# The layout of 2 KB of row scales on their way through DRAM, in a one-core decoder layer

## The chip, the cores and the metric

The kernel runs on one core of one Trainium2 chip, in one launch. The metric is the device time of an execution in microseconds, lower is better. Its engines are named as in the profile: PE (TensorE, matrix products; PEld is its weight load), DVE (VectorE), ACT (ScalarE), POOL (GpSimd) and SP (SyncE, which in this kernel issues every DMA transfer).

## The reference

One decoder layer over 2048 tokens of width 1024, float32. An input projection feeds two groups: a differential attention of 8 heads, and a gated linear recurrence of the same width. Their outputs, each with a SiLU gate, are joined, projected, normalised and added to the input. The change touches the end of the attention only, the RMS norm of each head's output over its 128 channels (the sub-norm):

```python
def rmsnorm(x, g):
    xf = x.astype(jnp.float32)
    y = xf * lax.rsqrt(jnp.mean(xf * xf, axis=-1, keepdims=True) + NORM_EPS)
    return (y * g.astype(jnp.float32)).astype(x.dtype)
...
o = diff_attention(qh, kh, vh, lam)
o = rmsnorm(o, subln_g[l]) * (1.0 - lam_init)
y_attn = o.reshape(B, S, ATTN_WIDTH).astype(x.dtype) * jax.nn.silu(g_attn)
...
y = jnp.concatenate([y_attn, y_lru], axis=-1)
y = jnp.einsum('bse,ed->bsd', y, w_out[l])
x = x + rmsnorm(y, post_norm_g[l])
```

So every (token, head) pair has one scale, the reciprocal root, by which 128 values are multiplied.

## The kernel before, in words

Matmuls take each float32 operand as a high and a low part, and three products replace one (`hi*hi`, `lo*hi`, `hi*lo`). The work runs in five stages.

1. Up to about 590 us: normalise and transpose the input, then project (L228, L530) and run the recurrence for tokens 0 to 1023. Everything that later stages need is stored in DRAM: `q_s`, `k_s`, `v_s`, `g_s`, `yl_s`.
2. To about 1125 us: `attention` for the token pairs 0 to 3 (a pair is 256 tokens), all 8 heads, with the projections of tokens 1024 to 2047 (`fill_proj`) woven in as filler for PE.
3. To about 1390 us: the recurrence of the second half; `load_wo` loads and splits the first blocks of `w_out`.
4. To about 2203 us: `attention` for pairs 4 to 7, with the output projection as filler (`fill_out`, L1048). It loads `y` from `ya_s` or `yl_s` (L958), splits it on POOL (L70, L71), loads partial sums (`part_s`, L1036 to L1044), adds them on DVE (L1058, one PSUM tile for all groups) and, for rows that are complete, runs `finish`: squares on ACT (L972), a product on POOL (L973), a reciprocal root on DVE (L979, L86 to L97), the residual (L983) and the store (L986). When the block of `w_out` changes, `load_wo` (L950) loads eight new pieces through two buffers, each split by POOL.
5. The rest: the output projection of the last 1024 rows (`right`, `left`, L1098).

`attention` goes through a list of slots, one per (head, pair, half, component). For each slot an order is written out by hand: loads of keys, values, queries and gates (L600, L606, L616, L623), the softmax exponentials (L683), then matmuls by a small clock model: scores (L642), transposes of the weights (L715, then ACT L719 and DVE L720), values (L738) and filler; last `combine` and the norm steps. The norm of a (head, 512 tokens) is cut into six steps over five slots: norm1 takes the squares on ACT and `yt`, the gated output, on DVE (L751); norm2 sums the squares over channels on PE (L760) and takes the reciprocal root on DVE (L75 to L82, called `f` in the profile). There the scales lie as 128 partitions x 4, token `t*128 + q` at partition q, column t, whereas `yt` has channels on its partitions and tokens along them. So the scales must be laid out along the free dimension and repeated on all 128 partitions. This is done through DRAM: norm3 (L773) writes 2 KB to `r_s`, norm4 (L777) reads them back with the same 2 KB for every partition into `rb`, norm5 (L782) multiplies on POOL, norm6 (L785) stores the result in `ya_s`. There are 8 heads x 4 = 32 such norms, 16 in stage 2 and 16 in stage 4.

All DMAs are issued by SP in the order in which the program states them. L777 waits there until the write of L773 has landed, and L785 until POOL's product is done.

Of the kernel before, what the change touches and what calls it, by code (L numbers as in the profile page):

```python
# [8 lines left out]
F32 = mybir.dt.float32  # L9
# [4 lines left out]
ALU = mybir.AluOpType  # L14
# [4 lines left out]
P = 128  # L19
# [3 lines left out]
H = 8  # L23
CH = 512
NJ = S // CH
# [18 lines left out]
def hymba_kernel(  # L44
# [6 lines left out]
    nc = tc.nc  # L51
# [5 lines left out]
    def grid(name, shape, a, b):  # L57
        return [[dram.tile(shape, F32, name=f"{name}{i}_{j}") for j in range(b)] for i in range(a)]
# [2 lines left out]
    k_s = grid("k_s", [64, 2, 2, CH], H, NJ)  # L61
    v_s = grid("v_s", [P, 2, 4, CH], 2, NJ)
    g_s = grid("g_s", [P, CH], H, NJ)
    r_s = grid("r_s", [4, P], H, NJ)
    ya_s = [dram.tile([P, H, CH], F32, name=f"ya_s{j}") for j in range(NJ)]
    yl_s = [dram.tile([P, NB, CH], F32, name=f"yl_s{j}") for j in range(NJ)]
    part_s = [[dram.tile([P, D], F32, name=f"part_s{r}_{i}") for i in range((8, 16)[r])] for r in range(2)]
# [524 lines left out]
    def attention(prs, kv_p, e_p, a_p, ps_s, ps_w, ps_o, nsb, fill, per_slot, kbufs, vbufs, p1bufs):  # L592
# [151 lines left out]
        nrm = {}  # L744
# [25 lines left out]
            nrm[h, j] = (f, yt)  # L770

        def norm3(h, j):
            nc.sync.dma_start(out=r_s[h][j].rearrange("t q -> q t"), in_=nrm[h, j][0][:, 2, :])  # L773

        def norm4(h, j):
            rb = a_p.tile([P, 4, P], F32, tag="sq", name="rb", bufs=1)
            nc.sync.dma_start(out=rb, in_=r_s[h][j].partition_broadcast(P))  # L777
            nrm[h, j] = (rb, nrm[h, j][1])

        def norm5(h, j):  # L780
            rb, yt = nrm[h, j]
            nc.gpsimd.tensor_tensor(out=yt, in0=yt, in1=rb.rearrange("p t q -> p (t q)"), op=ALU.mult)  # L782

        def norm6(h, j):
            nc.sync.dma_start(out=ya_s[j][:, h, :], in_=nrm.pop((h, j))[1])  # L785
# [9 lines left out]
        for p in range(H * NS):  # L795
            h, pr = p // NS, prs[p % NS]
# [35 lines left out]
        for s in range(U + 12):  # L832
# [49 lines left out]
            run("N1", norm1)  # L882
            run("N2", norm2)
            run("N3", norm3)
            run("N4", norm4)
            run("N5", norm5)
            run("N6", norm6)
        for _ in fill:
# [12 lines left out]
    with ExitStack() as pa:  # L901
        kv_p = pa.enter_context(tc.tile_pool(name="kvA", bufs=2))
        e_p = pa.enter_context(tc.tile_pool(name="expA", bufs=2))
        a_p = pa.enter_context(tc.tile_pool(name="attA", bufs=2))
# [106 lines left out]
    with ExitStack() as pb:  # L1011
        kvB_p = pb.enter_context(tc.tile_pool(name="kvB", bufs=2, side="right"))
        e_p = pb.enter_context(tc.tile_pool(name="expB", bufs=2, side="right"))
        a_p = pb.enter_context(tc.tile_pool(name="attB", bufs=2, side="right"))
# [153 lines left out]
```

## Time and profile before

| | |
|---|---|
| median of 3 runs | 2303.52 us (2302.61 to 2305.75) |
| profiled execution, its own time | 2302.22 us |
| its span, first to last instruction | 2300.4 us |
| granted clock of PE, mean | 0.98 |
| busy: PE, DVE, ACT, POOL | 2183.5, 1482.6, 984.2, 804.7 us |
| moved by DMA | 317.94 MB, 138 GB/s |

In rows of the profile, `x32` is a count; a row of a timeline gives start, duration, engine, line, operation and `out<-in`, and in square brackets how long the engine was idle before it and who ended that. A row of waits gives the total, the number of times and the longest. A row of a time window gives the window, its length, the busy time of PE, PEld, DVE, ACT and POOL, the granted clock, the busy share of the DMA engines and their GB/s. "DMA to landing" is the time from a transfer's issue to its completion.

### The profile page before, as it was taken

To read this page: it belongs to the slowest core of one execution; us is meant where nothing else is said; L and a number is where in the kernel's file an instruction comes from. 1 tells how busy PE (TensorE), PEld (TensorE's weight loads), DVE (VectorE), ACT (ScalarE), POOL (GpSimd) and SP (SyncE) were. 2 spreads that over 40 slices of the span, in tenths; PEclk is the share of its full clock that TensorE was granted. 3 is DMA by queue.
4 is the path that set the end of the run, shared out by engine and by line. 5 is a ranking of instruction groups with operands and counts; after the bars stand their busy time and mean duration, and the time that the engine had idled before them with its cause. 6 is when DMAs were issued, how large, how long until landed. Compare 5 with 4: busy or idle time off the path is not lost. (4 is left out here: it accounts for less than half of the span.)

```text
span 2300.4 us, 31837 instructions
## 1 busy us (share of the span) xinstructions
PE 2183.5 (95%) x11281; PEld 1800.9 (78%) x11281; DVE 1482.6 (64%) x2976; ACT 984.2 (43%) x2227; POOL 804.7 (35%) x773
## 2 busy tenths in 40 slices
PE   7999999999899999999989998999999998999778
PEld 6888888888678878888878775888788886887666
DVE  6532145456576666666237786888888887888565
ACT  4311134434443444444125564665555655555211
POOL 1222034444311111111266553233533335345452
PEclk9999999999999999999999998999999999999989
DMA  6554322332569876864452117456466475655473
GB/s 201 155 150 149 112 86 85 105 106 69 141 155 188 169 172 175 183 165 116 128 179 67 60 37 185 105 138 169 112 156 165 111 147 135 173 138 142 113 258 128
DMA packets 358785, 317.94 MB, mean 138 GB/s; under 512 B 32546, under 2 KB 290659, under 8 KB 358627
## 3 DMA queue, kind: packets, MB, share of 16 engines
q1 hardware_dynamic: 358626, 315.91, 52.8%
q8 instruction: 89, 1.46, 0.3%
q14 instruction: 70, 0.57, 0.1%
HBM read 221.41 MB, written 94.44 MB: 137 GB/s over the span
## 5 line engine op out<-in xcount | busy, mean ns | idle before, releaser
L228 PE MATMUL ps<-hh,whi 128*128 128x512 f32 (+1 forms) x1456 | 569.6, 391 | 2.7 <-DVE hilo L245 2.0
L228 PE MATMUL ps<-hh,wlo 128*128 128x512 f32 (+1 forms) x1456 | 567.4, 390 | 0.0
L228 PE MATMUL ps<-hl,whi 128*128 128x512 f32 (+1 forms) x1456 | 565.2, 388 | 1.1 <-DVE hl L446 1.1
L683 ACT ACTIVATE p<-s,nm 128x512 f32<-128x512 f32 (+3 forms) x640 | 392.1, 623 | 328.7 <-DVE nm L667 220.4
L665 DVE TENSOR_REDUCE mx<-s 128x1 f32<-128x512 f32 (+3 forms) x576 | 341.0, 617 | 114.9 <-PE s L642 96.3
L642 PE MATMUL s<-ks,qs 128*128 128x512 f32 (+2 forms) x1280 | 369.7, 387 | 28.9 <-DMA ks<-k_s 16.8
L200 POOL TENSOR_TENSOR wlo<-wraw,whi 128x1024 fp32r<-128x1024 f32 x88 | 222.7, 2531 | 437.3 <-DVE whi L199 133.3
L228 PEld LDWEIGHTS ps<-hh,whi 128*128 128x128 f32 x1456 | 277.6, 191 | 53.6 <-DVE hilo L245 2.4
L228 PEld LDWEIGHTS ps<-hl,whi 128*128 128x128 f32 x1456 | 277.2, 190 | 52.7 <-DVE hl L446 1.4
L228 PEld LDWEIGHTS ps<-hh,wlo 128*128 128x128 f32 x1456 | 276.6, 190 | 51.1
L642 PEld LDWEIGHTS s<-ks,qs 128*128 128x128 f32 x1280 | 216.4, 192 | 82.3 <-ACT p L683 33.0
L719 ACT ACTIVATE wh<-pw 128x512 fp32r<-128x512 f32 (+1 forms) x288 | 160.3, 577 | 186.5 <-PE pw L715 183.0
L738 PE MATMUL o<-wh,vs 128*128 128x256 f32 (+1 forms) x1152 | 222.5, 283 | 0.0
L720 DVE TENSOR_TENSOR wl<-pw,wh 128x512 fp32r<-128x512 f32 (+1 forms) x288 | 185.4, 653 | 35.8 <-ACT wh L719 34.3
L738 PEld LDWEIGHTS o<-wh,vs 128*128 128x128 f32 x1152 | 193.2, 191 | 18.1 <-ACT wh L719 2.1
L70 POOL TENSOR_SCALAR yh<-yraw 128x256 fp32r<-128x256 f32 x196 | 92.3, 488 | 290.6 <-PE f L1048 267.9
L1048 PE MATMUL f<-woh,yh 128*128 128x512 f32 x392 | 163.2, 416 | 25.0 <-DVE yv L1058 17.9
L782 POOL TENSOR_TENSOR yt<-yt,rb 128x512 f32<-128x512 f32 x32 | 44.1, 1379 | 405.4 <-DMA rb<-r_s 218.7
L701 DVE SCALAR_TENSOR_TENSOR p<-p,rr,p 128x128 f32<-128x128 f32 (+15 forms) x128 | 179.2, 1400 | 2.8
L715 PE MATMUL pw<-ident,p 128*128 128x128 f32 x1088 | 169.4, 274 | 5.8 <-DVE wl L720 4.5
L738 PE MATMUL o<-wl,vs 128*128 128x256 f32 x576 | 163.7, 284 | 8.9 <-DVE wl L720 8.9
L1048 PE MATMUL f<-wol,yh 128*128 128x512 f32 x392 | 163.3, 417 | 0.9 <-POOL wol L71 0.9
(166 smaller groups left out, 3298.7 us busy)
## 6 DMA issues: line engine op xcount, KB each, us to landing
wraw<-in_w_in_dram SPq DMA_DIRECT2D x96, 512.0 KB, 4.8
qs<-q_s SPq DMA_DIRECT2D x128, 256.0 KB, 5.2
vs<-v_s SPq DMA_DIRECT2D x48, 512.0 KB, 6.2
ks<-k_s SPq DMA_DIRECT2D x96, 256.0 KB, 5.5
xt<-in_x_dram SPq DMA_DIRECT2D x32, 512.0 KB, 4.7
k_s<-hilo SPq DMA_DIRECT2D x64, 256.0 KB, 4.2
q_s<-hilo SPq DMA_DIRECT2D x64, 256.0 KB, 3.5
v_s<-hilo SPq DMA_DIRECT2D x32, 512.0 KB, 3.7
```

The costliest lines, as they stand in the source:

```text
L70: nc.gpsimd.tensor_scalar(out=hi, in0=src, scalar1=1.0, scalar2=1.0, op0=ALU.mult, op1=ALU.mult)
L200: nc.gpsimd.tensor_tensor(out=lo, in0=src, in1=hi.bitcast(F32), op=ALU.subtract)
L228: nc.tensor.matmul(out=ps[:, t0:t0 + n], lhsT=a[:, k, :], rhs=b[:, k, t0:t0 + n], start=(k == 0 and m == 0), stop=(k == KC - 1 and m == 2),)
L642: nc.tensor.matmul(out=ps[:, b0 - c0:b0 - c0 + nk], lhsT=qq[:, c, t * P:(t + 1) * P], rhs=kst[h, b0 // CH][:, c, 0:nk], start=(m == 0), st ...
L665: nc.vector.tensor_reduce(out=mx[:, pi:pi + 1], in_=sc[u, pi][:, 0:c1 - c0], axis=AX.X, op=ALU.max)
L683: nc.scalar.activation(out=p[:, c0:c1], in_=sc.pop((u, pi))[:, 0:c1 - c0], func=AF.Exp, bias=negm[u], accum_out=acc,)
L701: nc.vector.scalar_tensor_tensor(out=p0[:, 0:n], in0=p1[:, 0:n], scalar=rr[:, 1:2], in1=p0[:, 0:n], op0=ALU.mult, op1=ALU.add,)
L715: nc.tensor.transpose(pw[:, i * P:(i + 1) * P], wts[h, pr, t][:, kb * P:(kb + 1) * P], ident)
L719: nc.scalar.activation(out=wh[:, 0:n], in_=pw[:, 0:n], func=AF.Copy)
L720: nc.vector.tensor_tensor(out=wl[:, 0:n], in0=pw[:, 0:n], in1=wh[:, 0:n].bitcast(F32), op=ALU.subtract,)
L738: nc.tensor.matmul(out=po[h, j][:, oo:oo + w1 - w0], lhsT=a[:, kb % 4, :], rhs=w[:, w0:w1], start=(kb == 0 and m == 0), stop=(kb == 2 * pr ...
L1048: nc.tensor.matmul(out=ps, lhsT=a[:, k, :], rhs=b, start=(k == 0 and m == 0), stop=(k == 7 and m == 2),)
```

## The change

`r_s` becomes partition-major: [128, 4] in place of [4, 128]. The write then puts the four scales of a partition next to one another, 16 bytes in one run; before, each scale went to a place 512 bytes from the next of its partition. The broadcast read is again 2 KB in one run per partition, but `rb` now holds them as 128 x 4, so the product on POOL reads `rb` with a step of four elements. `yt` stays as it is, seen as 4 x 128.

```diff
-    r_s = grid("r_s", [4, P], H, NJ)
+    r_s = grid("r_s", [P, 4], H, NJ)
...
         def norm3(h, j):
-            nc.sync.dma_start(out=r_s[h][j].rearrange("t q -> q t"), in_=nrm[h, j][0][:, 2, :])
+            nc.sync.dma_start(out=r_s[h][j], in_=nrm[h, j][0][:, 2, :])

         def norm4(h, j):
-            rb = a_p.tile([P, 4, P], F32, tag="sq", name="rb", bufs=1)
+            rb = a_p.tile([P, P, 4], F32, tag="sq", name="rb", bufs=1)
             nc.sync.dma_start(out=rb, in_=r_s[h][j].partition_broadcast(P))
             nrm[h, j] = (rb, nrm[h, j][1])

         def norm5(h, j):
             rb, yt = nrm[h, j]
-            nc.gpsimd.tensor_tensor(out=yt, in0=yt, in1=rb.rearrange("p t q -> p (t q)"), op=ALU.mult)
+            y4 = yt.rearrange("p (t q) -> p t q", t=4)
+            nc.gpsimd.tensor_tensor(out=y4, in0=y4, in1=rb.rearrange("p q t -> p t q"), op=ALU.mult)
```

## The prediction

> **What bounds the kernel now.** I read the page first (busy shares, transfers, chain), then the SyncE queue's own waits, then the rows of the two lines that the change touches, and last the timelines around every idle stretch of TensorE (PE) that can be followed back to them.
>
> ```profile
> PE 2183.5 (95%) x11281; PEld 1800.9 (78%) x11281; DVE 1482.6 (64%) x2976; ACT 984.2 (43%) x2227; POOL 804.7 (35%) x773
> ...
> DMA packets 358785, 317.94 MB, mean 138 GB/s; under 512 B 32546, under 2 KB 290659, under 8 KB 358627
> ...
> PE ps_y L1098 3%; DMA r_s<-f 1%; DMA yraw<-ya_s 1%; DMA out_dram<-xt 0%; DMA yv<-part_s 0%; DVE w3l L204 0%; DMA rb<-r_s 0%; PE f L1048 0%; DMA xt<-in_x_dram 0%; DVE xt L983 0%; DVE w3h L203 0%; DVE f L81 0%; PE s L642 0%; DVE f L82 0%; DVE f L80 0%
> ```
>
> PE is busy 2183.5 us; against the span of 2300.4 us that leaves 117 us in which it idles; but for the pace of the matmuls themselves, no change of transfers can win more. The share lines of the chain name a tiny transfer, `r_s<-f` (2 KB), second.
>
> The SyncE queue's waits, in total, times, longest:
>
> ```profile
> SPq L777 <- DMA r_s<-f: 242.2, 32, 9.8
> ...
> SPq L785 <- POOL yt L782: 163.5, 32, 8.2
> ```
>
> SyncE issues every transfer in program order. Per norm (32 of them) it stands 242.2 / 32 = 7.6 us at L777 until the write of L773 has landed, because the broadcast read needs it, and 5.1 us more at L785 for the product. Everything later in the program that must be loaded stands behind.
>
> The rows of the lines, durations in ns and the landing times of their transfers:
>
> ```profile
> L773 SPq DMA_DIRECT2D r_s<-f x32: 367/376/1200, 661.3 to 2173.6; - x32
> ...
> DMA to landing us min/median/max: 7.6/9.0/11.0
> ```
>
> ```profile
> L782 POOL TENSOR_TENSOR yt<-yt,rb x32: 1261/1290/2151, 679.0 to 2187.0; 128x512 f32<-128x512 f32 x32
> L785 SPq DMA_DIRECT2D ya_s<-yt x32: 319/320/337, 680.3 to 2188.3; - x32
> ...
> DMA to landing us min/median/max: 2.0/2.1/4.2
> ```
>
> A 2 KB write takes 9.0 us, while L785 stores 256 KB, in 128 rows of 2 KB, in 2.1 us. So neither bytes nor a fixed cost of any write explains the 9.0: what differs is 512 pieces of 4 bytes. The trace also shows that others pay for it:
>
> ```profile
> 2139.50:2147.50 8.00, 7.66 (x48) 6.76 (x48) 5.78 (x16) 2.39 (x4) 0.00 (x0) 0.87 0.94 33
> ```
>
> In the 8 us behind the write issued at 2137.45 (its row stands below) the DMA engines count as 0.94 busy and move 33 GB/s, against a mean of 138. The write thus costs twice: SyncE waits for it, and transfers already issued behind it crawl.
>
> **The change, part by part.** *The write (L773).* Before, the DRAM side runs over t outermost, so each of 4 x 128 scales is a piece of its own; 32 writes x 512 = 16,384 of the 32,546 packets under 512 B. After, a partition's four scales lie side by side: 128 pieces of 16 bytes. No row shows a 16-byte piece. Bounds: at best it lands like the L785 store with its 128 pieces, 2.0 (saving 7.6 - 2.0 = 5.6 by the minima, 6.9 by the medians); at worst a 16-byte piece costs four 4-byte ones, and nothing is saved; nothing excludes a loss of a fraction of a us. I take the price as going with the number of pieces: of the excess 7.6 - 2.0 = 5.6 a quarter stays, 1.4, and **4.2 us are saved per write**. I trust this value since the only write with 128 pieces lies at 2.0, so the count separates the two rows that are there.
>
> The Trainium skill (DMA: Bandwidth & Descriptors, Specifications) says that transfers under 512 B are done as read-modify-write. By it 16 bytes are in the same class as 4, so it promises nothing from the larger piece, only from fewer of them; the excess of the 4-byte write in these rows agrees with the class, and whether one such piece is dearer when it has 16 bytes no row here shows.
>
> *The read (L777).* Still 2 KB of contiguous DRAM for each partition, one issue, same bytes: nothing. It is issued as much earlier as the write lands.
>
> *The product (L782).* Now reads `rb` at a step of 16 bytes. Before, 1.29 us at the median and 2.15 at worst. No POOL row has such a step, so I bound the extra by 0 and 2.15 - 1.29 = 0.86, and take the middle, 0.43. Who waits for it is SyncE at L785 and POOL's own splits behind it, so on the path it eats 0.4 of the 4.2 wherever the way leads through L782 or L785; 32 x 0.43 = 14 us more of POOL are hidden under its 65% of idle time.
>
> The Trainium skill (GPSIMD Engine Reference, Performance pitfalls for Q7 kernels) speaks against the edit: a read step over 8 bytes costs about half as much again per element. An estimate by it is 1.29 x 1.5 = 1.94 us, 0.65 more instead of 0.43, and the sum below would be under 1 us smaller.
>
> *Where the 4.2 us reach PE.* Five places, by the timelines. First norm:
>
> ```profile
> 661.31 0.37 SPq L773 DMA_DIRECT2D r_s<-f  x1
> ...
> 664.18 0.39 SPq L195 DMA_DIRECT2D wraw<-in_w_in_dram  x1
> ...
> 677.99 0.69 DVE L199 CAST whi<-wraw 128x1024 fp32r<-128x1024 f32 x1 [7.22 <-DMA wraw<-in_w_in_dram]
> 679.33 0.39 PE L738 MATMUL o<-wl,vs 128*128 128x256 f32 x1 [2.31 <-DVE wl L720]
> ```
>
> The weights issued behind the write take 677.99 - 664.18 = 13.8 us; DVE waits 7.22 for them, and the next DVE instruction releases PE after 2.31 idle. 4.2 earlier closes it: **-2.3**.
>
> The last norm of the first half:
>
> ```profile
> 1122.53 0.37 SPq L773 DMA_DIRECT2D r_s<-f  x1
> 1123.16 0.32 SPq L266 DMA_DIRECT2D g_s<-st  x1
> ...
> 1131.86 0.32 SPq L777 DMA_DIRECT2D rb<-r_s  x1
> ...
> 1134.59 0.60 ACT L924 ACTIVATE vt<-ps 128x512 f32<-128x512 f32 x1 [5.34 <-DMA g_s<-st]
> 1135.24 0.66 PE L928 MATMUL pv<-ident,vt 128*128 128x128 f32 x4 [1.19 <-ACT vt L924]
> ...
> 1139.07 0.32 SPq L785 DMA_DIRECT2D ya_s<-yt  x1
> ...
> 1151.98 0.60 ACT L243 ACTIVATE hilo<-ps 128x512 fp32r<-128x512 f32 x1 [7.99 <-DMA v_s<-hilo]
> ...
> 1153.36 0.50 PE L228 MATMUL ps<-hh,whi 128*128 128x512 f32 x1 [2.02 <-DVE hilo L245]
> ```
>
> The `g_s` store issued behind the write at 1123.16 holds its buffer until ACT may start at 1134.59, 11.4 us, and the stores queued after L785 come late; both gaps, 1.19 and 2.02, fit into 4.2 - 0.4: **-3.2**.
>
> The second half, where `w_out` is changed:
>
> ```profile
> 1892.01 0.61 SPq L773 DMA_DIRECT2D r_s<-f  x1
> ...
> 1905.08 1.28 POOL L782 TENSOR_TENSOR yt<-yt,rb 128x512 f32<-128x512 f32 x1 [13.73 <-DMA rb<-r_s]
> ...
> 1934.12 1.11 SPq L600 DMA_DIRECT2D ks<-k_s  x2
> ...
> 1940.45 0.77 PE L642 MATMUL s<-ks,qs 128*128 128x256 f32 x2 [10.04 <-DMA ks<-k_s]
> ```
>
> POOL idles 13.73 us for the broadcast, then splits `y` and the eight `w_out` blocks, whose loads SyncE issues one by one as POOL frees their buffers, and only then the `ks` load can be issued, at 1934.12; PE idles 10.04 us for it. POOL starts 4.2 - 0.4 earlier: **-3.8**; the gap stays open at 6.
>
> ```profile
> 2082.04 0.39 SPq L773 DMA_DIRECT2D r_s<-f  x1
> ...
> 2097.47 0.32 SPq L785 DMA_DIRECT2D ya_s<-yt  x1
> ...
> 2098.32 0.45 SPq L1042 DMA_DIRECT2D yv<-part_s  x1
> ...
> 2101.92 0.63 ACT L972 ACTIVATE junk<-yv 128x512 f32<-128x512 f32 x1 [2.79 <-DMA yv<-part_s]
> ...
> 2103.37 0.74 PE L642 MATMUL s<-ks,qs 128*128 128x512 f32 x2 [2.52 <-ACT p L683]
> ```
>
> Write, product, `yv` load, ACT, PE stand in a line: ACT's wait of 2.79 fits into 3.8, and with it PE's whole gap goes: **-2.5**.
>
> The tail, by the chain that ended last and PE's timeline:
>
> ```profile
> 2137.45 10.26 DMA r_s<-f
> ...
> 2173.56 7.74 DMA r_s<-f
> ```
>
> ```profile
> 2152.39 0.77 PE L1048 MATMUL f<-woh,yh 128*128 128x512 f32 x1 [3.21 <-DVE yv L1058]
> ...
> 2195.42 0.77 PE L1048 MATMUL f<-woh,yh 128*128 128x512 f32 x1 [12.20 <-DVE yv L1058]
> ```
>
> Both last writes lie on that chain, with PE gaps of 3.21 and 12.20 behind them; the way of the first leads on through the product (4.2 - 0.4), that of the second leaves SyncE before L785 (4.2): **-8.0**. The 12.20 shrinks to 8.
>
> Sum: 2.3 + 3.2 + 3.8 + 2.5 + 8.0 = 19.8 us. Against it stands that loads which move up meet other loads, and that a slot in which PE no longer waits reaches the next late buffer sooner; I let a sixth go, 3 us, and take **17 us**. The profiled execution took 2302.22 us, 1.3 under the median of 2303.52, with 2 us around its span. 2303.5 - 17 = 2286.5; forecast **2286 us**.
>
> **The rivals.** *A, only the tail is on a path.* PE is at 95%, and 26 of the 32 writes have no PE gap behind them that I can follow to them; if the four earlier places merely move their wait to the next late buffer, 8 us remain: 2295. For it: those 26. Against: the gaps quoted have nothing else in their chain.
>
> *B, more than the sum.* Other transfers, too, run free of the crawl, at 5.6 instead of 4.2 per write (1.4 each for the three writes whose gaps stay open, at 1892 and in the tail: 4 us), and a matmul after a gap runs at a lower granted clock for a while:
>
> ```profile
> 1940.50:1943.80 3.30, 3.30 (x14) 3.01 (x15) 2.38 (x9) 1.79 (x6) 0.00 (x0) 0.53 1.11 216
> ```
>
> At 0.53 for 3.30 us a gap costs 1.5 us beyond itself; closed gaps at 679, 1153, 2103 and 2152 would give back up to 6. 2303.5 - 20 - 4 - 6 = 2273.
>
> *C, the piece is dear by its bytes.* Four scales in one piece cost as much as four pieces: the write stays at 9.0, the product is 0.4 to 0.9 later at the three or four places behind it: 2303.5 to 2307, no change that shows. For it: no 16-byte row. Against: a row of 2 KB costs less than any.
>
> *D, slower: the strided product.* One mechanism at L782: if it takes over 1.29 + 4.2 = 5.5 us, 4.3 times as long, POOL gives back more than the write saves, and SyncE stands at L785 for it. At 8 us, 2.5 lost at each of the four places on the way through L782: 2303.5 + 10 = 2313. Nothing in the trace comes near that for 512 elements.
>
> **How the numbers follow.** Forecast 0.51, A 0.17, B 0.14, C 0.12, D 0.06. A measurement of this kernel tells 0.2%, 4.6 us, from no change. The forecast, A and B are faster by more: 0.82; C with a rest of the small gains is the same: 0.12; D slower: 0.06. C and D are the 0.18 left out of the range; it reaches from just under B, 2270, to above A, 2300.
>
> **What would show it.** The write's landing median between 3 and 6 us (the one step on which all hangs); SyncE's total at L777 down to 242 - 32 x 4.2 = 108 us; packets under 512 B down by 32 x 384 = 12,288, to some 20,300; the product at 1.3 to 2.2 us; PE's busy time equal within 5 us, its gaps at 679, 1153 and 2103 gone, those at 1940 and 2195 about 4 us shorter. Wrong: a landing still near 9, a product above 4 us, or the same SyncE gain with PE's gaps at other places.

## The result, and the profile after

The changed kernel takes 2267.6 us (2263.72 to 2267.95) against 2303.52 (2302.61 to 2305.75): a ratio of 0.9845, interval 0.9833 to 0.9857. That is 36 us less where 17 were forecast, and 2.4 us below the low end of the range. The profiled execution of after has a span of 2265.8 us (before 2300.4) at a mean granted clock of 0.986 (0.980). From L782 on, each line of before is one further down: the product is L783, the store L786.

The page of after: busy time of the engines, packets, and the share line of the chain, which no longer names `r_s<-f`.

```profile
PE 2177.7 (96%) x11281; PEld 1796.7 (79%) x11281; DVE 1486.9 (66%) x2976; ACT 986.5 (44%) x2227; POOL 809.8 (36%) x773
...
DMA packets 346496, 317.94 MB, mean 140 GB/s; under 512 B 20257, under 2 KB 278370, under 8 KB 346338
...
PE ps_y L1099 3%; PE f L1049 0%; DVE w3l L204 0%; DMA yraw<-ya_s 0%; DVE xt L984 0%; PE o L738 0%; DMA yv<-part_s 0%; PE pw L715 0%; DVE f L80 0%; DVE ss L97 0%; PE s L642 0%; DVE f L81 0%; DMA out_dram<-xt 0%; DVE ss L96 0%; DVE f L82 0%
```

SyncE's waits at the two lines, and the rows of the write and the product (min/median/max):

```profile
SPq L786 <- POOL yt L783: 116.7, 30, 8.0
SPq L777 <- DMA r_s<-f: 60.3, 26, 5.2
```

```profile
L773 SPq DMA_DIRECT2D r_s<-f x32: 319/326/607, 660.5 to 2147.5; - x32
...
DMA to landing us min/median/max: 1.4/2.5/6.2
```

```profile
L783 POOL TENSOR_TENSOR yt<-yt,rb x32: 1533/1550/1583, 671.9 to 2152.9; 128x512 f32<-128x512 f32 x32
```

At the median the write lands after 2.5 us instead of 9.0 and the product takes 0.26 us more; the two waits of SyncE fall from 405.7 us together to 177.0. The broadcast read (L777), of the same 2 KB, lands after 3.7 us instead of 4.5.

To find where PE gained, a stretch around each of the five places of the prediction is bounded by the same two PE instructions in both traces. Each row gives the window, its length, the busy time of PE, PEld, DVE, ACT and POOL, the granted clock, the DMA share and the GB/s. Before, then after:

```profile
672.00:686.60 14.60, 12.29 (x63) 9.63 (x61) 7.15 (x13) 4.04 (x10) 3.61 (x2) 0.88 0.74 193
1125.90:1203.90 78.00, 70.56 (x302) 57.23 (x301) 23.12 (x27) 15.47 (x23) 47.60 (x47) 0.96 0.60 172
1928.00:1955.60 27.60, 17.56 (x101) 15.15 (x100) 17.13 (x38) 9.14 (x27) 13.97 (x22) 0.81 0.81 169
2022.70:2115.10 92.40, 86.39 (x501) 70.87 (x500) 79.13 (x173) 47.06 (x133) 47.98 (x64) 0.98 0.58 156
2131.70:2196.80 65.10, 41.13 (x202) 33.76 (x201) 37.04 (x87) 13.35 (x33) 30.57 (x41) 0.84 0.56 143
```

```profile
671.20:681.30 10.10, 10.10 (x63) 8.28 (x61) 6.76 (x13) 4.14 (x10) 3.92 (x2) 1.00 0.68 186
1121.90:1192.70 70.80, 68.96 (x301) 56.47 (x300) 22.42 (x27) 15.61 (x23) 47.12 (x46) 0.98 0.64 190
1918.70:1939.70 21.00, 17.75 (x101) 15.28 (x100) 16.13 (x37) 9.19 (x27) 8.36 (x14) 0.92 0.81 190
2006.80:2092.90 86.10, 83.66 (x501) 70.16 (x500) 77.79 (x173) 47.24 (x133) 51.20 (x64) 1.00 0.58 167
2109.50:2163.00 53.50, 41.22 (x203) 33.81 (x202) 38.69 (x86) 13.46 (x33) 29.77 (x41) 0.87 0.57 171
```

The lengths differ by 4.5, 7.2, 6.6, 6.3 and 11.6 us: 36.2 us, where the span shrank by 34.6, so in sum all of the gain lies in the five stretches, and the rest of the span comes out 1.6 longer. Length less PE's busy time is PE's idle time: it falls by 2.3, 5.6, 6.8, 3.6 and 11.7, in sum 30.0. The other 6.2 are the same matmuls done in less busy time, and they come from the stretches whose quoted gaps closed (2.2, 1.6 and 2.7 in the first, second and fourth); where a gap stays open, in the third and the last, busy time grows by 0.2 and 0.1. The first row shows it best: a gap of 2.31 is closed, but 4.5 us are won, because the 63 matmuls need 10.10 us in place of 12.29, at a clock of 1.00 in place of 0.88. Two windows of before, inside that place, show where the clock was lost:

```profile
681.00:682.50 1.50, 1.50 (x7) 1.21 (x6) 1.33 (x2) 0.10 (x2) 1.50 (x1) 0.50 0.62 199
682.50:684.00 1.50, 1.50 (x4) 1.13 (x4) 1.37 (x3) 0.06 (x1) 0.14 (x1) 0.50 0.86 245
```

PE waited until 679.33 and then, from 681 to 684, ran at half its clock. The Trainium skill (TensorE: Matmul & The Clock Gate, Part 1) says that the clock gate has two states, half and full speed, set by how busy PE was in a free-running window of about 3.4 us, with half speed after an idle window. The trace agrees on the half, 0.50, for some 3 us; it differs in that an idle stretch of 2.31 us, shorter than such a window, was enough here.

Rows of the timeline at the open gaps. First of after, then of before, one that the prediction does not show:

```profile
1918.18 1.11 SPq L600 DMA_DIRECT2D ks<-k_s  x2
...
1924.40 0.58 PE L642 MATMUL s<-ks,qs 128*128 128x256 f32 x2 [3.25 <-DMA ks<-k_s]
...
2129.32 0.47 PE L1049 MATMUL f<-woh,yh 128*128 128x512 f32 x1 [0.81 <-DVE yv L1059]
...
2151.93 0.76 PE L1049 MATMUL f<-woh,yh 128*128 128x512 f32 x1 [4.61 <-DVE yv L1059]
...
2162.20 0.47 PE L1049 MATMUL f<-woh,yh 128*128 128x512 f32 x1 [2.29 <-DVE yv L1059]
```

```profile
2177.52 0.47 PE L1048 MATMUL f<-woh,yh 128*128 128x512 f32 x1 [2.50 <-DVE yv L1058]
```

The gaps of 10.04 and 12.20 are 3.25 and 2.29 now. Counted by the matmuls between them, the gap of 3.21 in the tail is the one of 0.81, and that of 2.50, between the two that the prediction quotes, has become 4.61. Ahead of the loads at 1918.18 the product starts 7.3 us behind the issue of its write (1882.29 to 1889.60) where it took 13.1 before, and what ends POOL's idle time there, 7.96 us, is DVE (L701), no longer the broadcast.

### The profile page after: what moved, and what is told of

Its sections match the earlier page's. It is cut to its first block, busy times and chain, and to the rows that moved or that the text cites. A ratio compares the mean times of both kernels' runs of the same rounds, so it can differ in the third digit from the quotient of the medians.

```text
span 2265.8 us, 31837 instructions
## 1 busy us (share of the span) xinstructions
PE 2177.7 (96%) x11281; PEld 1796.7 (79%) x11281; DVE 1486.9 (66%) x2976; ACT 986.5 (44%) x2227; POOL 809.8 (36%) x773
## 2 busy tenths in 40 slices
DMA packets 346496, 317.94 MB, mean 140 GB/s; under 512 B 20257, under 2 KB 278370, under 8 KB 346338
## 5 line engine op out<-in xcount | busy, mean ns | idle before, releaser
L701 DVE SCALAR_TENSOR_TENSOR p<-p,rr,p 128x128 f32<-128x128 f32 (+15 forms) x128 | 184.1, 1438 | 2.8
L1049 PE MATMUL f<-woh,yh 128*128 128x512 f32 x392 | 162.5, 415 | 12.2 <-DVE yv L1059 7.7
L1049 PE MATMUL f<-woh,yl 128*128 128x512 f32 x392 | 162.3, 414 | 0.0
```

Source lines behind the costliest of these rows:

```text
L701: nc.vector.scalar_tensor_tensor(out=p0[:, 0:n], in0=p1[:, 0:n], scalar=rr[:, 1:2], in1=p0[:, 0:n], op0=ALU.mult, op1=ALU.add,)
L1049: nc.tensor.matmul(out=ps, lhsT=a[:, k, :], rhs=b, start=(k == 0 and m == 0), stop=(k == 7 and m == 2),)
```

## The experiments

Two questions were open. What makes the old write dear: the **number** of its pieces (the prediction's assumption), their **size**, or that pieces lie side by side (**neighbours**)? And how does its landing time cost the kernel: because SyncE stands (**waiting**), or because transfers behind it crawl (**crawl**)? The kernel before took 2309 to 2312 us on the chips of these runs, against 2303.5 in the result above, while the changed kernel stays near 2266; the gain is 43 us here and 36 there, and why is not shown. So kernels are compared by their ratio to it, or directly where they ran on one chip.

**The product alone.** The tokens' scales come out permuted.

```diff
 # kernel before
-            rb = a_p.tile([P, 4, P], F32, tag="sq", name="rb", bufs=1)
+            rb = a_p.tile([P, P, 4], F32, tag="sq", name="rb", bufs=1)
...
-            nc.gpsimd.tensor_tensor(out=yt, in0=yt, in1=rb.rearrange("p t q -> p (t q)"), op=ALU.mult)
+            nc.gpsimd.tensor_tensor(out=y4, in0=y4, in1=rb.rearrange("p q t -> p t q"), op=ALU.mult)
```

> The kernel before with its old write (512 pieces of 4 bytes), but the product reads rb at a step of 16 bytes; so each token gets another token's scale. Theory (the write alone made the gain, the product costs its 0.26 us per norm and nothing behind it): product 1.29 to 1.55 us, write's landing median stays 9, time 2302 to 2306. Rival (a strided POOL read disturbs DVE or holds SyncE): time over 2308.

2312.59 us (2309.57 to 2318.23), ratio 1.0012, interval 0.9998 to 1.0025. Its product takes 1.555 us at the median, its write lands in 8.4/9.6/12.2 us: the strided read costs 0.26 us each, and nothing in the kernel's time that shows.

**The write alone.** The product reads `rb` at unit step, so the scales are permuted.

```diff
 # changed kernel
-            nc.gpsimd.tensor_tensor(out=y4, in0=y4, in1=rb.rearrange("p q t -> p t q"), op=ALU.mult)
+            nc.gpsimd.tensor_tensor(out=yt, in0=yt, in1=rb.rearrange("p q t -> p (q t)"), op=ALU.mult)
```

> The changed kernel with the write partition-major, but the product reads rb flat at unit step; so each token gets another token's scale. Theory: product back at 1.29 us, landing median 2.5 us, time 2265 to 2268, at most 2 us under the changed kernel's 2267.6. Rival (the strided product costs on the path): 2258 to 2263.

2265.62 us (2264.73 to 2267.53), ratio 0.9805, interval 0.9782 to 0.9828. The changed kernel itself, run once more beside later experiments, has the same ratio:

> The changed kernel itself, to be compared with the others of this call on one chip: 2264 to 2272, ratio 0.981 to 0.986.

2266.37 us (2263.4 to 2273.45), ratio 0.9805, interval 0.9791 to 0.9819. The whole gain comes from the write.

**What makes a small write dear.** A kernel without the layer writes to DRAM from the same small tile, eight kinds of write in turn. The first form was:

```diff
+            nc.sync.dma_start(out=dst, in_=src)      # one of eight kinds, six times each
+            nc.sync.dma_start(out=back, in_=b)       # reads one word of it back
```

> No layer: zeros are stored, then eight kinds of small write from 128 partitions to DRAM, six times each, one after the other with nothing else under way. old: 512 pieces of 4 bytes, the layout before. new: 128 of 16 bytes. far: 512 of 4 bytes, each 64 bytes from the next. few: 128 of 4 bytes next to one another. fewfar: 128 of 4 bytes, 64 bytes apart. many16: 512 of 16 bytes. eight: 256 of 8 bytes. own: 512 of 4 bytes, partition-major with a gap of 4 bytes. Landing of old 7.6, of new 1.4. Theory number (each piece costs, whatever its size): old, far, many16, own about 7.6, eight 3 to 4, few, fewfar, new 1.4 to 2. Theory size (pieces of 4 bytes are dear, of 16 cheap): many16 under 3, few 2 to 3, far and own 7.6. Theory neighbours (pieces of different partitions in one 64-byte line get in each other's way): far under 4, own under 5, few 3 or more, fewfar 1.4 to 2, many16 up to 4.

166.5 us in all. The writes were not kept apart by the read-backs, so landing times of one kind hold those of another, and nothing follows. In the second form the word goes back into the source tile, so that each write must land before the next starts:

```diff
-            nc.sync.dma_start(out=back, in_=b)
+            nc.sync.dma_start(out=f[0:1, 2, 0:1], in_=b)
```

> No layer: zeros are stored, then the eight kinds of small write (old: 512 pieces of 4 bytes as before; new: 128 of 16; far: 512 of 4, 64 bytes apart; few: 128 of 4, adjacent; fewfar: 128 of 4, 64 bytes apart; many16: 512 of 16; eight: 256 of 8; own: 512 of 4, partition-major, 4 bytes apart), six times, each followed by a read of one element back into the source, so that nothing overlaps; the time from a write's issue to the read's issue is its landing. Theory number (each piece costs, whatever its size): old, far, many16, own about 7.6, eight 3 to 4, few, fewfar, new 1.4 to 2. Theory size (4 bytes are dear, 16 cheap): many16 under 3, few 2 to 3, far and own 7.6. Theory neighbours (pieces of different partitions in one 64-byte line get in each other's way): far under 4, own under 5, few 3 or more, fewfar 1.4 to 2, many16 up to 4.

SyncE's waits for the eight kinds (total, times, longest), and their landing times:

```profile
SPq L98 <- DMA old_w<-f: 54.3, 6, 10.7
SPq L98 <- DMA few_w<-f: 44.9, 6, 9.1
SPq L98 <- DMA own_w<-f: 20.5, 6, 4.2
SPq L98 <- DMA eight_w<-f: 16.9, 6, 3.7
SPq L98 <- DMA many_w<-f: 14.0, 6, 2.6
SPq L98 <- DMA far_w<-f: 9.3, 6, 1.9
SPq L98 <- DMA new_w<-f: 7.3, 6, 1.7
SPq L98 <- DMA fewfar_w<-f: 6.6, 6, 1.3
```

| kind | pieces x bytes | pieces in 64 bytes of DRAM | landing min/median/max, us |
|---|---|---|---|
| old (layout before) | 512 x 4 | 16 | 8.5/9.2/11.1 |
| few | 128 x 4 | 16 | 7.2/7.6/9.4 |
| own (every other word) | 512 x 4 | 8 | 3.3/3.9/4.8 |
| eight | 256 x 8 | 8 | 2.8/3.0/4.1 |
| many | 512 x 16 | 4 | 2.6/2.7/3.0 |
| new (layout after) | 128 x 16 | 4 | 1.4/1.4/2.1 |
| far | 512 x 4 | 1 | 1.8/1.9/2.2 |
| fewfar | 128 x 4 | 1 | 1.4/1.4/1.6 |

A quarter of the pieces, still side by side, saves only 1.6 us (few); all 512, but 64 bytes apart, land in 1.9 (far). So number alone falls, and size falls with it (4 bytes in far and fewfar are cheap): the price follows first of all how densely the pieces lie. The 64 bytes of the table are only its yardstick; no run shows a border there. At an equal density four times as many pieces add 0.5 us (far against fewfar), 1.3 (many against new) and 1.6 (old against few). The Trainium skill (DMA: Bandwidth & Descriptors, Specifications) puts every transfer under 512 B in one class, done as read-modify-write; all eight kinds belong to it and land between 1.4 and 9.2 us, so the class alone does not set the price here. Spacings between 8 and 64 bytes were not tried with 4-byte pieces, and what in the path of the write makes neighbours slow stays open.

**Halfway.** 256 pieces of 8 bytes, which gives a write between the two in number and in density, and so does not part these (the write and `rb` follow the new shape):

```diff
 # changed kernel
-    r_s = grid("r_s", [P, 4], H, NJ)
+    r_s = grid("r_s", [2, P, 2], H, NJ)
...
-            nc.gpsimd.tensor_tensor(out=y4, in0=y4, in1=rb.rearrange("p q t -> p t q"), op=ALU.mult)
+            nc.gpsimd.tensor_tensor(out=y4, in0=y4, in1=rb.rearrange("p a q b -> p a b q"), op=ALU.mult)
```

> The changed kernel with the scales in two halves: 256 pieces of 8 bytes, and the product reads at a step of 8 bytes. Theory number: landing minimum 2.5 to 3.5, median 4 to 5, and the time between the two kernels, about 2275 to 2285. Theory size with its border at 4 bytes: landing as with 16 bytes (minimum 1.4 to 2), time 2265 to 2270. Product: 1.29 us if a step of 8 bytes is free, 1.55 if any step costs.

2273.27 us (2268.81 to 2276.99), ratio 0.9836, interval 0.982 to 0.9852: 7 us above the changed kernel on the same chip, with intervals that just part, and between the two ranges expected. Landing 3.1/4.1/6.2; the product, and the five places between the same PE instructions (to 0.1 us):

```profile
L783 POOL TENSOR_TENSOR yt<-yt,rb x32: 1289/1308/1690, 673.1 to 2154.9; 128x512 f32<-128x512 f32 x32
```

```profile
671.20:681.40 10.20, 10.20 (x63) 8.38 (x62) 6.90 (x13) 4.24 (x11) 3.66 (x2) 1.00 0.64 179
1120.20:1193.10 72.90, 69.57 (x303) 56.62 (x302) 23.41 (x27) 15.47 (x23) 47.58 (x47) 0.98 0.64 184
1916.80:1939.60 22.80, 18.79 (x100) 16.14 (x98) 16.76 (x38) 9.78 (x29) 8.82 (x16) 0.85 0.79 179
2006.90:2092.90 86.00, 83.58 (x501) 70.00 (x499) 77.89 (x173) 46.94 (x132) 50.96 (x64) 1.00 0.58 167
2109.50:2164.70 55.20, 39.91 (x201) 32.67 (x201) 37.62 (x86) 13.20 (x33) 29.45 (x41) 0.91 0.59 168
```

This write saves 9.0 - 4.1 = 4.9 us, near the prediction's 4.2, and yet the five places shrink by 4.4, 5.1, 4.8, 6.4 and 9.9 = 30.6 us (24.7 of idle time and 5.9 of busy time), where the prediction had 19.8. With 4.9 its own rules would give 8.0 for the closed gaps and 3 x 4.9 for the three open ways, 22.7. So 7.9 of the 10.8 us missed here are not the size of the saving. (The profiled execution, 2268.81 us, is the fastest of the four, and the trace of before is from another chip.)

The Trainium skill (GPSIMD Engine Reference, Performance pitfalls for Q7 kernels) sets the border of a dear read at a step of 8 bytes. The trace agrees on the border: 1.308 us at 8 bytes, 1.291 at unit step in the write alone. At 16 bytes it is 1.55, 20% more, where the Trainium skill has 50%.

**Waiting without crawl.** Before the broadcast read, three more copies from DRAM to DRAM, each awaited, none with 4-byte pieces:

```diff
 # changed kernel
+    b_s = [grid(f"b{i}_s", [P, 4], H, NJ) for i in range(3)]
...
+            at = r_s[h][j]
+            for b in b_s:
+                nc.sync.dma_start(out=b[h][j], in_=at)
+                at = b[h][j]
-            nc.sync.dma_start(out=rb, in_=r_s[h][j].partition_broadcast(P))
+            nc.sync.dma_start(out=rb, in_=at.partition_broadcast(P))
```

> The changed kernel, but the 2 KB of scales goes through three more DRAM to DRAM copies, each awaited by SyncE, before the broadcast read: SyncE and the broadcast are some 6 us later per norm with no 4-byte piece. Theory wait: 2290 to 2303, SyncE's total at the norm's read near 242 us or more. Theory crawl: 2267 to 2275. Both: 2278 to 2290.

2290.76 us (2289.29 to 2301.77), ratio 0.992, interval 0.9896 to 0.9943. SyncE's waits:

```profile
SPq L791 <- POOL yt L788: 120.6, 32, 6.3
SPq L780 <- DMA r_s<-f: 54.9, 25, 5.1
SPq L780 <- DMA b_s<-r_s: 50.3, 24, 5.1
SPq L782 <- DMA b_s<-b_s: 36.7, 21, 3.4
SPq L780 <- DMA b_s<-b_s: 27.6, 26, 2.1
```

54.9 + 50.3 + 36.7 + 27.6 = 169.5 us where after has 60.3: 109 more, and 96 more issues, the 64 of the second and third copy at 0.5 us each. The waits stay under the 242 us that were expected. All this costs 25 us against the write alone (2265.62, same chip), with no 4-byte piece. Lateness is dear by itself; but the broadcast and the product come later here too, and the run does not part SyncE's standing from that.

**Crawl without waiting.** Two first tries add the old write as one that nobody awaits:

```diff
 # changed kernel, first try (crawl_only): behind the read of rb
+            nc.sync.dma_start(out=x_s[h][j].rearrange("t q -> q t"), in_=nrm[h, j][0][:, 2, :])
 # second try (crawl_late): behind the store of ya_s
+            nc.sync.dma_start(out=x_s[h][j].rearrange("t q -> q t"), in_=f[:, 2, :])
```

> The changed kernel, and right behind the issue of each broadcast read one more write of the same scales in the old layout (512 pieces of 4 bytes) to a scratch that nobody reads and SyncE does not wait for. Theory wait (the gain is SyncE's freed 5.7 us per norm at L777): 2267 to 2273. Theory crawl (the gain is that transfers issued behind the 4-byte write no longer stand in the queues for 7 us): 2285 to 2303. Both: some 2278 to 2285.

2299.97 us (2295.55 to 2304.07), ratio 0.9954, interval 0.9938 to 0.997.

> The changed kernel, with one more write of the scales in the old layout (512 pieces of 4 bytes) to a scratch that nobody reads, issued behind the store of the product, so that SyncE's waits for the norm stay as in the changed kernel (L777 60 us, L786 117 us in total). Theory crawl: transfers issued behind it lose some 6 us each time, 2285 to 2300. Theory wait: 2267 to 2273.

2303.21 us (2295.58 to 2306.16), ratio 0.9974, interval 0.9961 to 0.9987. Both had a flaw: in their traces the extra write is issued ahead of the read of `rb` (in 31 and 28 of the 32 norms), so that this read crawls too (7.7 and 7.4 us at the median, 3.7 in after) and SyncE waits for the product behind it. In the first:

```profile
SPq L788 <- POOL yt L785: 232.4, 31, 13.8
SPq L778 <- DMA r_s<-f: 96.7, 24, 9.9
```

232.4 at the product, in place of 116.7, is waiting again; the two are mixed. The third try writes from `yt` itself, which holds the write behind the store, and its twin spreads the pieces by 64 bytes:

```diff
 # changed kernel, crawl_behind
+            nc.sync.dma_start(out=x_s[h][j].rearrange("t q -> q t"), in_=yt[:, 0:4])
 # far_behind: x_s = grid("x_s", [4, P, 16], H, NJ)
+            nc.sync.dma_start(out=x_s[h][j][:, :, 0].rearrange("t q -> q t"), in_=yt[:, 0:4])
```

> The changed kernel, with one write of 512 pieces of 4 bytes (four columns of the product, to a scratch that nobody reads) right behind the store of the product, where it depends on the product and so cannot move ahead of the broadcast read. SyncE's waits for the norm stay near those of the changed kernel (60 and 117 us). Theory crawl: what is issued behind it loses some 6 us 32 times, 2283 to 2303. Theory wait: 2267 to 2273.

2351.31 us (2348.47 to 2354.05), ratio 1.0174, interval 1.016 to 1.0189: 85 us above the changed kernel on the same chip, slower than before and far above both ranges. Its waits at the norm, the rows behind one extra write, and one stretch of `attention`, followed by the same stretch of after:

```profile
SPq L788 <- POOL yt L784: 125.2, 31, 7.4
SPq L778 <- DMA r_s<-f: 82.7, 25, 6.6
```

```profile
778.63 0.43 SPq L789 DMA_DIRECT2D x_s<-yt  x1
...
789.75 0.75 DVE L752 SCALAR_TENSOR_TENSOR yt<-o,csub,gt 128x512 f32<-128x512 f32 x1 [8.65 <-DMA x_s<-yt]
...
791.86 0.69 ACT L684 ACTIVATE p<-s,nm 128x512 f32<-128x512 f32 x1 [9.43 <-DVE nm L668]
...
792.69 1.12 PE L643 MATMUL s<-ks,qs 128*128 128x512 f32 x2 [5.14 <-ACT p L684]
```

```profile
709.60:811.60 102.00, 93.86 (x502) 77.05 (x501) 62.77 (x160) 39.00 (x102) 16.47 (x8) 0.97 0.85 161
```

```profile
700.10:791.00 90.90, 90.60 (x502) 74.51 (x501) 61.99 (x161) 39.26 (x102) 16.57 (x8) 1.00 0.70 182
```

SyncE's waits at the norm are only 31 us longer than in after (207.9 against 177.0), and yet the same work takes 11.1 us more, with the DMA engines at 0.85 and fewer GB/s. The rows show why in this stretch: SyncE does not wait for the extra write, but DVE does, because the write still reads `yt` when DVE is to fill it for the next norm. DVE stands 8.65 us, ACT's exponentials come late, and PE idles 5.14. Over the whole run DVE waits so 22.2 us, in 6 places. So here, too, waiting and crawl are mixed. PE's waits for the exponentials over the whole run, here and in after (total, times, longest):

```profile
PE s L643 <- ACT p L684: 31.6, 16, 6.0
```

```profile
PE s L642 <- ACT p L683: 7.8, 10, 1.7
```

> The changed kernel with the same extra write of 512 pieces of 4 bytes behind the store of the product as in the run that took 2351 us, at the same place and with the same dependency, but each piece 64 bytes from the next. Theory neighbours: 2266 to 2275, nothing behind it crawls. Theory number (512 pieces or one more issue cost it): 2330 to 2355.

2274.42 us (2271.52 to 2282.88), ratio 0.9849, interval 0.9827 to 0.987. The same 512 pieces, 64 bytes apart, cost 0.0044 of 2310, 10 us over the changed kernel, against 85. By the ratios 75 us come from the addresses alone. That adjacent 4-byte pieces also hold up what is issued behind them shows in the DMA rate: in the stretch from 0.5 to 8.5 us behind each of the 32 extra writes it is 64 GB/s in the mean with adjacent pieces and 186 with spread ones. How the 75 us divide between this crawl and DVE's wait for `yt`, of which far_behind has none, is not shown.

**Whether more is to be had.** SyncE still stands 116.7 us at L786. Three edits aim at it:

```diff
 # changed kernel, later_steps
-                later(s0 + 11, "N4", h, pr // 2)
+                later(s0 + 12, "N4", h, pr // 2)
...
-                later(s0 + 13, "N6", h, pr // 2)
+                later(s0 + 14, "N6", h, pr // 2)
 # store_on_pool, store_on_act
-            nc.sync.dma_start(out=ya_s[j][:, h, :], in_=nrm.pop((h, j))[1])
+            nc.gpsimd.dma_start(...)    # the same store, issued by POOL
+            nc.scalar.dma_start(...)    # or by ACT
```

> The changed kernel with the broadcast read and the product in the slot after (both at s0+12) and the store one slot later (s0+14), so that SyncE finds the write landed and the product done. SyncE's waits at these lines fall from 60 and 117 us to under 20 and 40. Theory wait (SyncE's remaining stand still reaches PE): 2255 to 2263. Theory crawl (what remains reaches PE little): 2264 to 2270.

2264.36 us (2263.51 to 2266.64), ratio 0.981, interval 0.9787 to 0.9833; the waits stay at 58.4 and 116.8 us, where under 20 and 40 were expected. The edit did not move the steps away from their waits, so it tests nothing.

> The changed kernel with the store of the product issued by POOL, which has just made it, in place of SyncE: SyncE does not wait at L786 (117 us before). Theory wait: 2257 to 2264. Theory crawl: 2264 to 2270, or slower by POOL's own work for 32 issues if that takes over 1 us each.

2278.27 us (2271.48 to 2289.8), ratio 0.9875, interval 0.9847 to 0.9902. SyncE's wait is gone, and yet the kernel is 14 us slower than the one above on the same chip, outside both ranges. POOL waits 167.1 us for the broadcast instead of 112.1; what makes it slower stays open.

> The changed kernel with the store of the product issued by ACT in place of SyncE, which then no longer waits for POOL at L786 (117 us in total). If SyncE's remaining wait reaches PE and ACT has room: 2255 to 2263, a version better than both. If ACT's own wait for the product delays the exponentials instead: 2270 to 2290.

2330.92 us (2324.81 to 2336.14), ratio 1.0083, interval 1.0062 to 1.0104, with PE's busy time up to 2194.2 us: slower than before and than both ranges. ACT now waits for the product, in front of the exponentials:

```profile
ACT p L683 <- POOL yt L783: 70.3, 16, 8.4
```

None of the three beats the changed kernel by more than its interval.

## Why the prediction was wrong in size and right in place

Right: the write was the cost; the gain lies around the five places named, and the rest of the span, taken together, won nothing; 20,257 packets under 512 B (forecast 20,300); the product at 1.55 us (forecast up to 2.2, 0.43 more taken, 0.26 measured); the gaps at 679, 1153 and 2103 went, and PE's gap for the keys and the last one shrank, though by 6.8 and 9.9 where some 4 were forecast for each. Rivals A, C and D fall by this. B, more than the sum, was nearest, and its two items were both there: the open ways gave more, and the pace of the matmuls 6.2 where it had up to 6, but not at all four places (the tail's busy time did not fall).

Wrong: 17 us. From the forecast to the 34.6 us by which the span shrank, with the places' own numbers:

| term as the prediction had it | forecast | measured | missed |
|---|---|---|---|
| "4.2 us are saved per write": price by number of pieces; idle time at the open gaps (1940 and the tail) | 3.8 + 8.0 | 6.8 + 11.7 | 6.7 |
| closed gaps worth their own length (679, 1153, 2103): idle time | 2.3 + 3.2 + 2.5 | 2.3 + 5.6 + 3.6 | 3.5 |
| pace of the matmuls behind a gap, left to rival B | 0 | 6.2 | 6.2 |
| "a sixth let go" for loads that meet others | -3 | -1.6 | 1.4 |

Two steps failed. **The price by the number of pieces.** By it a quarter of the excess stays; few and far contradict it both ways (7.6 us with 128 pieces, 1.9 with 512). Landing fell by 6.5 us at the median, to 2.5 where 3 to 6 were expected, near the 6.9 kept as the upper end. The broadcast read, taken at nothing, landed 0.8 sooner as well. A step of 6.5, less 0.26 for the product where the way leads through it, gives 6.2 at 1940 and 12.7 in the tail; 6.8 and 11.7 were measured. In the tail that nearness is luck. The first way was taken at 3.8, more than the gap of 3.21 that it was to close; up to the end of that gap PE won only 0.9 (from 20.69 us, 2131.70 to 2152.39, to 19.82, 2109.50 to 2129.32), since 2.4 less idle time was nearly eaten by 1.5 more busy time, at a clock of 0.83 in place of 0.90. The rest, 10.7, came behind it, where 4.2 were forecast. The two rows compared, 512 x 4 bytes and 128 x 2 KB, differed in number, size and spacing at once, and the count was read off them as if it were alone.

**"Where the 4.2 us reach PE".** Each place was sized by PE's own gap. Halves shows that this failed even with about the assumed saving: 30.6 us in the five places. Behind a gap the clock falls to 0.50, so a closed gap gives back busy time too, 5.9 us in halves and 6.2 in after. This had a row in the prediction, but stood with a rival instead of in the sum. Gaps that the prediction did not list shrank too: from 1126 to 1204 idle time falls by 5.6, not by 1.19 + 2.02, because a gap of 4.23 at 1190.55 (L316) is 1.84 now.

SyncE's total at L777 was to fall to 108 us; it fell to 60.3, and the wait for the product by 46.8 more, which had not been counted; the time at each stop depends on how early SyncE comes. PE's busy time was to stay within 5 us; it fell by 5.8.

Of the two costs that the prediction gave the write, both exist: lateness without 4-byte pieces costs 25 us in wait_only, and behind the extra writes of crawl_behind the DMA rate falls to a third of that in far_behind. In the kernel before they fall in the same 7 us, since SyncE issues nothing while it stands. How much crawls there differs: from 0.4 us behind the write's issue to the read's, the DMA engines move 0 to 162 GB/s, 69 in the mean of the 32, so the row of 33 that the prediction shows is not typical. Behind the last write, where PE's gap shrank most, nothing else was under way before:

```profile
2173.50:2181.40 7.90, 5.41 (x24) 4.20 (x23) 3.47 (x11) 0.72 (x2) 3.50 (x5) 1.00 0.03 0
```

There the write landed late, after 7.7 us, with the DMA engines at 0.03, and waiting alone was paid. At the rate of wait_only, 25 us for 109 of waits and 48 of issues, the 229 us of waits that the change removed would be worth 36 of the 44 us that the write alone gained on that chip. That is an estimate; no run parts the two over the whole kernel in the old order of issue.

## What to carry to other kernels

Ask of a small DRAM write how densely its pieces lie: let each partition write what it holds in one run, and pay for it with a strided read where that engine has time, or leave 64 bytes between single words (no run here reads such a layout back for every partition). Place such a write where no load stands right behind it and no engine needs its source tile soon, since its landing time is paid by whoever is queued next as well as by whoever awaits it. When a gap of PE closes whole, count the half-clock stretch behind it in the sum, and size a place by the window between two fixed PE instructions, not by the one gap that is quoted.

## What the hardware showed that was not expected

Number and price of pieces part company: 512 single words 64 bytes apart land in 1.9 us, 128 words side by side in 7.6. A 2 KB write of adjacent words that SyncE does not wait for, 32 times, costs the kernel 85 us, 42 us more than the old kernel paid for its 32 awaited ones, while the same words spread out cost 10. With nothing else under way such a write still takes 7.7 us, with the DMA engines 0.03 busy. POOL's product takes 1.31 us at a step of 8 bytes against 1.29 at unit step, and 20% longer at 16.
